# First modulation as rows in TensorE's column groups, later modulations held behind it, and an unused tile of 128 bytes

## The chip, the cores and the metric

The kernel runs on one core of a Trainium2 chip. The metric is the device time of one execution in microseconds (us), here as the median of three runs. Beside the runs, one execution was recorded by the hardware profiler; all durations below come from that record. Engines are called as in the profile: PE is TensorE, DVE is VectorE, ACT is ScalarE, POOL is GpSimd, SP is SyncE, whose queue issues the DMAs here.

## The reference

One layer of a decoder trunk, all in fp32, over 1024 positions of width 1024. A vector `c` gives six vectors that scale, shift and gate the two halves of the layer:

```python
cond = jax.nn.silu(c)
mod = cond @ ada_w[l] + ada_b[l]
sh1, sc1, g1, sh2, sc2, g2 = [m[:, None, :] for m in jnp.split(mod, 6, axis=-1)]
h = rmsnorm(x, ln1_g[l]) * (1 + sc1) + sh1
(a_val, a_gate, b_q, b_k, b_v, b_g, b_lr,
 c_q, c_k, c_v, d_u, d_v) = jnp.split(h @ w_in[l], splits, axis=-1)
...
mix = jnp.concatenate([o_a, o_b, o_c, o_d], axis=-1).astype(dt) @ w_out[l]
x = x + g1 * mix
h = rmsnorm(x, ln2_g[l]) * (1 + sc2) + sh2
x = x + g2 * conv_ffn(h, ffn_up[l], ffn_conv_w[l], ffn_conv_b[l], ffn_down[l])
return rmsnorm(x, lnf_g)
```

The four outputs `o_a` to `o_d` are a convolution of 31 taps, a gated linear attention, a dilated attention and a spatial gate; `conv_ffn` is an up-projection to 2 x 2816, a convolution of three taps, a gate and a down-projection. "The first modulation" below is the pair `sh1`, `sc1`; "the later ones" are the other four vectors.

## The kernel before

**Matrix products.** Each fp32 matrix is split into a high part, rounded to TensorE's fp32r format, and a low part, the rest (ACT makes the high part at L70, POOL or DVE the low one at L71). A product is then three fp32r matmuls: low x high, high x low, high x high (L92 to L94 in the first part of the kernel, L1221 to L1223 in `chain_mm` of the feed-forward part). `h_t` are tiles of 512 columns with activations or left operands, `wh_t` tiles with weights; in the feed-forward part `ht_t` are 24 further tiles of 512 columns that hold sums of blocks and the down-projection's operands. They are allocated in the pool `ph2`, and stand in a matmul either as the moving operand (`ht_t,wh_t` in a row's names) or as the weights of the array (`h_t,ht_t`).

**The start.** The eight row tiles of `x` are loaded in two halves (g = 0 and 1, four tiles each). `norm1` makes their squares' sums (ACT, two of the tiles on DVE), a reciprocal root by Newton steps on DVE (L77 to L82), and scales the rows (L249 on ACT, L251 on DVE). `norm1_T` transposes them on TensorE, a block of 128 columns at a time (L264), and ACT or DVE (L288) copies the transposed blocks to `xrT`. `modulate` then applies scale and shift: the high part `hH` straight on ACT (L318), the fp32 value in place (L322 on ACT for g = 0, L320 on DVE for g = 1), and the low part `hL` on POOL as their difference (L323). `first` multiplies `hH` and `hL` with the weights of the convolution and its gate (L331), 168 matmuls of 512 columns, accumulated over the eight blocks k as these come.

**The modulation.** Scale and shift of a block k are 128 elements each along the partitions. They are made in five pieces, `ADA_1` = (0), (1), (2, 3), (4, 5), (6, 7), so that the first blocks can start before the whole of `ada_w` is there. For a piece p, `ada_mac` multiplies blocks of `ada_w` by the elements of `cond` and adds them up on DVE (L222 for the first, L224 for the others), `ada_sum` sums the result over the partitions on TensorE with a column of ones as the moving operand (L304; for p = 0 the first four of the eight k go to TensorE directly, with a column of `cond`), and `ada_mod` adds the bias and one and multiplies by the norm's gain (L310 to L312). The order is written out by hand: `with after(...)` holds back what is queued inside it until a named instruction has been issued.

**The later modulations** are made by `ada_rest` with the same products on DVE (L826, L828), from 256-column blocks that share the buffers of tag `k2` with the accumulators of the first; a scheduler interleaves them with the projections. Two such accumulators are begun at 61.87 us, ahead of the convolution's taps on DVE (L464, L471).

## Time and profile before

| | us |
|---|---|
| median of three runs | 1170.57 |
| lowest and highest run | 1168.76, 1171.06 |
| the profiled execution | 1173.14 |
| its span | 1171.4 |
| TensorE busy | 1120.8 (96% of the span) |
| DVE busy | 810.9 (69%) |
| POOL busy | 707.6 (60%) |
| ACT busy | 561.8 (48%) |

The profiled execution took 1173.14 us, of which the span from the first to the last recorded instruction is 1171.4 us. Its mean granted clock of TensorE is 0.990 of full speed. TensorE is the busiest engine by far, and over the whole span the others have room; but these are means over parts with different limits, and in a short part at the start another engine can be the one that is full. In the rows below, the idle time in brackets is that of the engine just ahead of the row, and the arrow names what ended it.

### The profile page before, as it was taken

The numbers are of one execution on the slowest core, as the hardware profiler recorded it, in microseconds if no ns is written. First come the engines' busy times: TensorE is split into PE (matmuls) and PEld (weight loads), VectorE is DVE, ScalarE is ACT, GpSimd is POOL, SyncE is SP. The second block draws the span as 40 slices with busy tenths as digits, with TensorE's granted clock in tenths as the row PEclk, the third lists the DMA queues.
The fourth block names the chain that finished last, engine by engine and source line by source line (L and its number), as shares of the span: only waits on it lengthen the run. The fifth ranks groups of instructions, "written<-read, shape, count | busy, mean of one in ns | idle before, by whom it ended". The sixth has DMA issues, their size and how long they took to land.

```text
span 1171.4 us, 16065 instructions
## 1 busy us (share of the span) xinstructions
PE 1120.8 (96%) x5686; PEld 917.0 (78%) x5686; DVE 810.9 (69%) x1321; ACT 561.8 (48%) x909; POOL 707.6 (60%) x487
## 2 busy tenths in 40 slices
PE   4889999999999999999999999999999999999996
PEld 4668987866797878877887888888887778888885
DVE  6998979376678865555576676857686766654547
ACT  5552235373331523367666555555554646443432
POOL 2565574221232346648978777867787737895963
PEclk9999999989999999999999999999999999999998
DMA  9632232031331534482134546445644488574533
GB/s 354 253 100 71 75 112 86 19 108 58 123 109 64 188 99 180 153 293 76 46 135 135 189 180 242 172 168 183 242 181 178 144 308 329 194 239 142 198 109 144
DMA packets 70145, 186.86 MB, mean 160 GB/s; under 512 B 8097, under 2 KB 9265, under 8 KB 70065
## 3 DMA queue, kind: packets, MB, share of 16 engines
q1 hardware_dynamic: 70064, 185.84, 45.3%
q8 instruction: 45, 0.74, 0.2%
q14 instruction: 36, 0.29, 0.1%
HBM read 141.50 MB, written 42.21 MB: 157 GB/s over the span
## 4 chain that ended last, share of the span: by engine, by line
PE 71%; DVE 6%; POOL 2%; issue 2%; ACT 2%; DMA 2%; SPq 0%; ACTq 0%; DVEq 0%; POOLq 0%
PE a_ps L1221 8%; PE a_ps L1223 8%; PE a_ps L1222 8%; PE s_ps L92 4%; PE s_ps L93 4%; PE s_ps L94 3%; PE e_ps L1221 3%; PE e_ps L1222 3%; PE e_ps L1223 3%; PE y_ps L1223 3%; PE y_ps L1222 3%; PE y_ps L1221 3%; PE c_ps L1223 2%; PE c_ps L1221 2%; PE c_ps L1222 2%
## 5 line engine op out<-in xcount | busy, mean ns | idle before, releaser
L71 POOL TENSOR_TENSOR wh_t<-wf_t,wh_t 128x512 fp32r<-128x512 f32 (+2 forms) x131 | 216.4, 1659 | 178.6 <-ACT wh_t L70 169.3
L70 ACT CAST wh_t<-wf_t 128x512 fp32r<-128x512 f32 (+2 forms) x135 | 98.0, 739 | 139.7 <-PE s_ps L93 35.1
L1114 DVE SCALAR_TENSOR_TENSOR y_ps<-x_t,col,y_ps 128x1023 f32<-128x1023 f32 x88 | 112.6, 1283 | 38.9 <-ACT y_ps L1112 38.1
L71 POOL TENSOR_TENSOR h_t<-m_t,h_t 128x512 fp32r<-128x512 f32 x70 | 102.3, 1476 | 39.2 <-ACT h_t L70 37.3
L71 DVE TENSOR_TENSOR ht_t<-m_t,ht_t 128x512 fp32r<-128x512 f32 x65 | 80.1, 1245 | 65.3 <-ACT ht_t L70 63.5
L1387 ACT COPY x_t<-a_ps 128x512 f32<-128x512 f32 x81 | 47.4, 585 | 79.5 <-PE a_ps L1223 79.4
L471 DVE SCALAR_TENSOR_TENSOR s_ps<-m_t,col,s_ps 128x512 f32<-128x512 f32 (+19 forms) x116 | 80.3, 740 | 1.1
L70 ACT CAST ht_t<-m_t 128x512 fp32r<-128x512 f32 x65 | 40.3, 620 | 78.2 <-DMA m_t<-ps 20.7
L71 POOL TENSOR_TENSOR wh_t<-m_t,wh_t 128x512 fp32r<-128x512 f32 x52 | 67.2, 1305 | 16.5 <-ACT wh_t L70 16.1
L1221 PE MATMUL a_ps<-h_t,wh_t 128*128 128x512 f32 x188 | 73.7, 392 | 1.7 <-ACT x_t L1240 1.0
L828 DVE SCALAR_TENSOR_TENSOR acc<-ad,cond,acc 128x256 f32<-128x256 f32 x112 | 68.8, 622 | 8.8 <-DMA ad<-in_ada 7.3
L1223 PE MATMUL a_ps<-h_t,wh_t 128*128 128x512 f32 x188 | 73.3, 390 | 0.0
L1222 PE MATMUL a_ps<-h_t,wh_t 128*128 128x512 f32 x188 | 73.3, 390 | 0.0
L680 POOL TENSOR_TENSOR m_t<-m_t,mx 128x128 f32<-128x128 f32 (+7 forms) x16 | 19.3, 1206 | 85.2 <-DVE mx L678 82.9
L1221 PE MATMUL a_ps<-ht_t,wh_t 128*128 128x512 f32 x176 | 69.5, 395 | 0.0
L1223 PE MATMUL a_ps<-ht_t,wh_t 128*128 128x512 f32 x176 | 69.5, 395 | 0.0
L1222 PE MATMUL a_ps<-ht_t,wh_t 128*128 128x512 f32 x176 | 69.4, 394 | 0.0
L93 PE MATMUL s_ps<-wh_t,h_t 128*128 128x512 f32 (+1 forms) x192 | 69.2, 361 | 0.0
L94 PE MATMUL s_ps<-wh_t,h_t 128*128 128x512 f32 (+1 forms) x192 | 68.9, 359 | 0.0
L92 PE MATMUL s_ps<-wh_t,h_t 128*128 128x512 f32 (+1 forms) x192 | 65.6, 368 | 1.0 <-DVE g1b L837 1.0
L1221 PE MATMUL e_ps<-h_t,wh_t 128*128 128x512 f32 x148 | 57.9, 391 | 0.9 <-POOL wh_t L71 0.9
L1222 PE MATMUL e_ps<-h_t,wh_t 128*128 128x512 f32 x148 | 57.7, 390 | 0.0
(344 smaller groups left out, 3356.5 us busy)
## 6 DMA issues: line engine op xcount, KB each, us to landing
m_t<-in_ffn_up SPq DMA_DIRECT2D x46, 512.0 KB, 4.8
ad<-in_ada SPq DMA_DIRECT2D x64, 256.0 KB, 3.4
ps<-m_t SPq DMA_DIRECT2D x22, 512.0 KB, 7.3
x_t<-in_ffn_down SPq DMA_DIRECT2D x22, 512.0 KB, 6.8
m_t<-ps SPq DMA_DIRECT2D x33, 256.0 KB, 4.3
x_t<-in_x SPq DMA_DIRECT2D x16, 512.0 KB, 6.3
wf_t<-in_w_out SPq DMA_DIRECT2D x16, 512.0 KB, 3.6
m_t<-in_ffn_down SPq DMA_DIRECT2D x28, 256.0 KB, 5.4
```

Source lines behind the costliest of these rows:

```text
L70: ac.copy(dst_h, src)
L71: return eng.tensor_tensor(dst_l, src, dst_h.bitcast(F32), op=ALU.subtract)
L92: pe.matmul(ps, ll, rh, start=first, stop=False)
L93: pe.matmul(ps, lh, rl, start=False, stop=False)
L94: return pe.matmul(ps, lh, rh, start=False, stop=last)
L471: ve.scalar_tensor_tensor(yA[t][:, o + a:e] if last else y[:, a:], h[:, o + a - s:e - s], cc(O_CW + (CONV_K - 1 - s) * 2 + t), y[:, a:], o ...
L828: ve.scalar_tensor_tensor(acc, f[:, kk, :], cond[:, k:k + 1], acc, op0=ALU.mult, op1=ALU.add)
L1114: ve.scalar_tensor_tensor(y[:, n:], z[:, :S - n], cc(O_FW + 88 - 44 * n + f), y[:, n:], op0=ALU.mult, op1=ALU.add)
L1221: pe.matmul(ps, ll, rh, start=start, stop=False, skip_group_check=True)
L1222: pe.matmul(ps, lh, rl, start=False, stop=False, skip_group_check=True)
L1223: return pe.matmul(ps, lh, rh, start=False, stop=stop, skip_group_check=True)
L1387: ac.copy(dict(P1=lo(za[f]), P6=hi(za[f]), P7=hi(zb), P4=lo(zb))[p], ba)
```

## The change

Three things are changed, and one or two that go with them.

In the first, `ada_mac` and `ada_sum` are replaced by `ada_rows`. The vector `cond` is copied 64 times side by side (`condr`), and stands as the weights of the array: 64 columns for p = 0 and 1, 32 columns for p = 2 to 4. A block of `ada_w`, 128 columns, is the moving operand. The output of a product lies on 64 or 32 partitions, so two or four column groups of the array each take their own 128 columns of `ada_w` and write their own partitions of one PSUM tile; every row in a group is the same. DVE copies the 128 x 128 result (L226 of the changed kernel), TensorE transposes it (L227), and every 64th or 32nd column of the transposed tile is a vector of the modulation. All eight k are done so, for every p.

In the same part, the in-place operation of `modulate` for g = 0 goes from ACT to DVE, and every second copy of a transposed block goes to DVE in place of every fourth. In the second, the first product of a later modulation is held until the last instruction of the latest `ada_mod` has been issued. In the third, the pool `ph2` gets one tile of 128 bytes per partition that nothing uses, ahead of its other tiles; `ht_t` and the 1024-column tiles `m4_t` then begin at multiples of 256 bytes (before, 128 bytes past one). `h_t` and `wh_t` begin at multiples of 256 bytes in both kernels.

```diff
@@ -200,7 +200,6 @@
     xt = [t_x() for _ in range(NT)]
     ada_t = {}
     SQ = ((1, 2), (1, 3))
-    PM = (4, 0, 0, 0, 0)
 
     def ada_load(p):
         ada_t[p] = []
@@ -215,14 +214,19 @@
         return ada_t[p][k // nk][:, k % nk, :]
 
 
-    def ada_mac(p):
-        acc = accs[p] = sm1.tile([P, 512], F32, tag="k2", name="acc1", bufs=N_K2)[:, :256 * len(ADA_1[p])]
-        for k in range(PM[p], KT):
-            if k == PM[p]:
-                r = ve.tensor_scalar(acc, ada_block(p, k), cond[:, k:k + 1], None, op0=ALU.mult)
-            else:
-                r = ve.scalar_tensor_tensor(acc, ada_block(p, k), cond[:, k:k + 1], acc, op0=ALU.mult, op1=ALU.add)
-        mac_last[:] = [r.ins]
+    def ada_rows(p):
+        n = 2 * len(ADA_1[p])
+        m, o = P // n, p % 2 * P
+        row, rows_T = sum_ps[:, o:o + P], sum_ps[:, 256 + o:256 + o + P]
+        for k in range(KT):
+            for c in range(n):
+                pe.matmul(row[m * c:m * c + m, :], condr[:, k, :m], ada_block(p, k)[:, c * P:(c + 1) * P],
+                          start=k == 0, stop=k == KT - 1)
+        rs = sm1.tile([P, 256], F32, tag="k1", name="rows", bufs=4)[:, :P]
+        ve.tensor_copy(rs, row)
+        r = pe.transpose(rows_T, rs, ident)
+        mods[p] = rows_T[:, 0:P:m]
+        return r.ins
 
     W1 = Weights([(w_a[k], 1024) for k in range(4)] + [(w_feat[FEAT_COLS.index(C_AG + P)], 1024)]
                  + [(w_feat[1], 1024), (w_feat[2], 1024), (w_tok[2, 0], 1024), (w_tok[2, 1], 1024), (w_feat[3], 1024), (w_feat[4], 1024)]
@@ -238,6 +242,8 @@
         x_load(i)
     ada_load(2)
     ac.activation(cond, cc(O_C, 8), AF.Silu)
+    condr = sm1.tile([P, 512], F32, tag="k2", name="condr", bufs=N_K2).rearrange("p (k m) -> p k m", k=KT)
+    ve.tensor_copy(condr, cond.unsqueeze(2).broadcast_to([P, KT, 64]))
     ve.tensor_scalar(adab1[:, 0, :], cc(O_AB + 8, 8), 1.0, None, op0=ALU.add)
     ve.tensor_scalar(adab1[:, 1, :], cc(O_AB + 32, 8), 1.0, None, op0=ALU.add)
 
@@ -285,41 +291,26 @@
     def norm1_T(g, ks):
         for k in ks:
             tp = norm_T(xt[4 * g:4 * g + 4], k, p_s)
-            (ve.tensor_copy if k in (3, 7) else ac.copy)(xrT[k][:, half(g)], tp)
+            (ve.tensor_copy if k % 2 else ac.copy)(xrT[k][:, half(g)], tp)
 
 
     hH = [[None, None] for _ in range(KT)]
     hL = [[None, None] for _ in range(KT)]
-    accs = {}
-    mac_last = []
-
-    def ada_sum(p):
-        for n in range(2 * len(ADA_1[p])):
-            c = 2 * ADA_1[p][0] + n
-            cs = slice(n * P, (n + 1) * P)
-            ms_ = [(ada_block(p, k)[:, cs], cond[:, k:k + 1]) for k in range(PM[p])]
-            if p in accs:
-                ms_.append((accs[p][:, cs], ones[:, 0:1]))
-            for i, (w, v) in enumerate(ms_):
-                r = pe.matmul(sum_ps[:, c:c + 1], w, v, start=i == 0, stop=i == len(ms_) - 1)
-        return r.ins
+    mods, mod_last = {}, []
 
     def ada_mod(p):
         t0, n = ADA_1[p][0], len(ADA_1[p])
-        tp, ks = sum_ps[:, 2 * t0:2 * (t0 + n)], slice(t0, t0 + n)
+        tp, ks = mods[p], slice(t0, t0 + n)
         ve.tensor_tensor(mod[:, 1, ks], tp[:, 0:n], cc(O_AB + t0, n), op=ALU.add)
         ve.tensor_tensor(mod[:, 0, ks], tp[:, n:2 * n], adab1[:, 0, ks], op=ALU.add)
-        ve.tensor_tensor(mod[:, 0, ks], mod[:, 0, ks], cc(O_L1 + t0, n), op=ALU.mult)
+        mod_last[:] = [ve.tensor_tensor(mod[:, 0, ks], mod[:, 0, ks], cc(O_L1 + t0, n), op=ALU.mult).ins]
 
     def modulate(ks, g):
         for k in ks:
             hf = xrT[k][:, half(g)]
             hH[k][g], hL[k][g] = t_h(), t_h()
             r = ac.activation(hH[k][g], hf, AF.Identity, bias=mod[:, 1, k:k + 1], scale=mod[:, 0, k:k + 1])
-            if g:
-                ve.tensor_scalar(hf, hf, mod[:, 0, k:k + 1], mod[:, 1, k:k + 1], op0=ALU.mult, op1=ALU.add)
-            else:
-                r = ac.activation(hf, hf, AF.Identity, bias=mod[:, 1, k:k + 1], scale=mod[:, 0, k:k + 1])
+            ve.tensor_scalar(hf, hf, mod[:, 0, k:k + 1], mod[:, 1, k:k + 1], op0=ALU.mult, op1=ALU.add)
             gp.tensor_tensor(hL[k][g], hf, hH[k][g].bitcast(F32), op=ALU.subtract)
         return r
 
@@ -334,19 +325,15 @@
 
     sum_ps = p_s()
     ve.memset(sum_ps, 0.0)
-    scaled = norm1(0)
+    ada_rows(0)
+    norm1(0)
     norm1_T(0, range(2))
-    with after(scaled):
-        ada_mac(0)
-        W1.split()
-        with after(*mac_last):
-            ada_mac(1)
-    ada_sum(0)
+    W1.split()
     wk = W1.get()
     ada_mod(0)
     r0 = modulate(ADA_1[0], 0).ins
     a_ps = [[p_s(), None] for _ in range(4)]
-    with after(ada_sum(1)):
+    with after(ada_rows(1)):
         f0 = first(wk, ADA_1[0], 0)
     ada_mod(1)
     modulate(ADA_1[1], 0)
@@ -362,7 +349,7 @@
             first(wk, ks, 0)
         if p == 1:
             ks = (0, 1)
-            scaled = norm1(1, r0)
+            norm1(1, r0)
             norm1_T(1, range(KT))
             for ft in range(3):
                 a_ps[ft][1] = p_s()
@@ -372,9 +359,7 @@
         with tc.issue_after(rounded.ins):
             W1.split()
         if p + 1 < len(ADA_1):
-            with after(*mac_last) if p > 1 else after(scaled):
-                ada_mac(p + 1)
-            ada_sum(p + 1)
+            ada_rows(p + 1)
         first(wk, ks, 1)
     W1.split()
 
@@ -823,7 +808,8 @@
                 for kk in range(2):
                     k = q * 2 + kk
                     if k == 0:
-                        ve.tensor_scalar(acc, f[:, kk, :], cond[:, 0:1], None, op0=ALU.mult)
+                        with after(*mod_last):
+                            ve.tensor_scalar(acc, f[:, kk, :], cond[:, 0:1], None, op0=ALU.mult)
                     else:
                         ve.scalar_tensor_tensor(acc, f[:, kk, :], cond[:, k:k + 1], acc, op0=ALU.mult, op1=ALU.add)
             if bc is not None:
@@ -1246,6 +1232,7 @@
 
 
     raw, tok = {}, {}
+    ph2.tile([P, 32], F32, name="pad")
 
     def token_rows(n):
 
```

On TensorE, the start of the program before reads as follows (the first number of a shape is partitions, the second columns; x12 is the number of such in a row; an fp32 product by a column counts once here and is two instructions in the trace):

```order
L304 MATMUL s_ps<-cond,m_t 128x1 x4
L264 MATMUL s_ps<-ident,x_t 128x128 x8
L304 MATMUL s_ps<-ones,acc_169 128x1
L304 MATMUL s_ps<-cond,m_t 128x1 x4
L304 MATMUL s_ps<-ones,acc_169 128x1
L304 MATMUL s_ps<-ones,acc_180 128x1 x2
L331 MATMUL s_ps<-h_t,wh_t 128x512 x12
L264 MATMUL s_ps<-ident,x_t 128x128 x11
L331 MATMUL s_ps<-h_t,wh_t 128x512 x8
L264 MATMUL s_ps<-ident,x_t 128x128
L331 MATMUL s_ps<-h_t,wh_t 128x512 x4
L264 MATMUL s_ps<-ident,x_t 128x128 x44
```

In the changed kernel the same place reads:

```order
L223 MATMUL s_ps<-m_t,condr 64x128 x16
L270 MATMUL s_ps<-ident,x_t 128x128 x8
L227 MATMUL s_ps<-ident,rows 128x128
L223 MATMUL s_ps<-m_t,condr 64x128 x16
L227 MATMUL s_ps<-ident,rows 128x128
L322 MATMUL s_ps<-h_t,wh_t 128x512 x12
L270 MATMUL s_ps<-ident,x_t 128x128 x12
L322 MATMUL s_ps<-h_t,wh_t 128x512 x12
L223 MATMUL s_ps<-m_t,condr 32x128 x5
L270 MATMUL s_ps<-ident,x_t 128x128 x12
L223 MATMUL s_ps<-m_t,condr 32x128 x27
L270 MATMUL s_ps<-ident,x_t 128x128 x12
```

The eight transposes of the first two blocks stand between the two first modulations' pieces in both. The sums of `acc` are gone, and with them what TensorE waits for on DVE; in their place stand 16 products of `ada_w` and `condr` per piece, and the third piece's 32 are broken up by transposes. Further on, the pieces of the changed kernel lie between the first projections (L331 before, L322 now):

```order
L322 MATMUL s_ps<-h_t,wh_t 128x512 x22
L223 MATMUL s_ps<-m_t,condr 32x128 x8
L223 MATMUL s_ps<-x_t,condr 32x128 x4
L322 MATMUL s_ps<-h_t,wh_t 128x512 x4
L223 MATMUL s_ps<-x_t,condr 32x128 x4
L223 MATMUL s_ps<-m_t,condr 32x128
L322 MATMUL s_ps<-h_t,wh_t 128x512 x16
L223 MATMUL s_ps<-m_t,condr 32x128 x7
L223 MATMUL s_ps<-x_t,condr 32x128 x8
L322 MATMUL s_ps<-h_t,wh_t 128x512 x18
L227 MATMUL s_ps<-ident,rows 128x128
L223 MATMUL s_ps<-m_t,condr 32x128 x8
```

Counting from the start, products of `condr` stand in nine unbroken blocks.

On DVE, the later modulations' first products stood as follows before, among the modulations of the second half (L320) and the fifth `ada_mod` (L310 to L312):

```order
L224 SCALAR_TENSOR_TENSOR acc_561<-x_t,cond,acc_561 128x512 x2
L826 TENSOR_SCALAR acc_1352<-ad_1353,cond 128x256
L828 SCALAR_TENSOR_TENSOR acc_1352<-ad_1353,cond,acc_1352 128x256
L828 SCALAR_TENSOR_TENSOR acc_1352<-ad_1357,cond,acc_1352 128x256
L320 TENSOR_SCALAR m_t<-m_t,mod 128x512
L828 SCALAR_TENSOR_TENSOR acc_1352<-ad_1357,cond,acc_1352 128x256
L828 SCALAR_TENSOR_TENSOR acc_1352<-ad_1389,cond,acc_1352 128x256
L310 TENSOR_TENSOR mod<-s_ps,col 128x2
L320 TENSOR_SCALAR m_t<-m_t,mod 128x512
L311 TENSOR_TENSOR mod<-s_ps,adab_63 128x2
L828 SCALAR_TENSOR_TENSOR acc_1352<-ad_1389,cond,acc_1352 128x256
L312 TENSOR_TENSOR mod<-mod,col 128x2
```

Now they stand behind the fifth `ada_mod` (L304 to L306 of the changed kernel):

```order
L313 TENSOR_SCALAR m_t<-m_t,mod 128x512 x3
L226 COPY rows<-s_ps 128x128
L313 TENSOR_SCALAR m_t<-m_t,mod 128x512
L304 TENSOR_TENSOR mod<-s_ps,col 128x2
L305 TENSOR_TENSOR mod<-s_ps,adab_63 128x2
L306 TENSOR_TENSOR mod<-mod,col 128x2
L812 TENSOR_SCALAR acc_1432<-ad_1433,cond 128x256
L812 TENSOR_SCALAR acc_1567<-ad_1568,cond 128x256
L814 SCALAR_TENSOR_TENSOR acc_1432<-ad_1433,cond,acc_1432 128x256
L814 SCALAR_TENSOR_TENSOR acc_1567<-ad_1568,cond,acc_1567 128x256
L313 TENSOR_SCALAR m_t<-m_t,mod 128x512
L814 SCALAR_TENSOR_TENSOR acc_1432<-ad_1437,cond,acc_1432 128x256 x2
```

The two accumulators of the later modulations (`acc_1352` and `acc_1487` before, `acc_1432` and `acc_1567` now) begin behind the last `mod`, and are filled in turns; the taps of the convolution follow behind them in both.

## Rows read from the trace of the kernel before

**Rows 1.** By stretch: length, busy time of each engine, PEclk, DMA, GB/s.

```profile
25.40:46.40 21.00, 15.59 (x98) 12.63 (x97) 20.01 (x38) 12.61 (x21) 7.24 (x4) 0.99 0.67 251
46.40:84.20 37.80, 33.50 (x146) 26.81 (x146) 37.12 (x46) 19.59 (x25) 26.64 (x17) 0.96 0.41 142
84.20:1171.40 1087.20, 1061.30 (x5406) 868.55 (x5406) 739.09 (x1198) 516.03 (x845) 668.25 (x457) 0.99 0.44 153
sum 1171.40, PE 1120.79 PEld 917.02 DVE 810.95 ACT 561.82 POOL 707.60; mean PE 224.16 PEld 183.40 DVE 162.19 ACT 112.36 POOL 141.52
```

**Rows 2.** Timeline of TensorE, 0 to 45 us: start, length, instruction, count, idle before.

```profile
21.59 1.01 PE L304 MATMUL s_ps<-ones,acc 128*128 128x1 f32 x4 [3.15 <-DVE acc L224]
22.47 4.36 PE L331 MATMUL s_ps<-h_t,wh_t 128*128 128x512 f32 x12
...
32.28 2.00 PE L264 MATMUL s_ps<-ident,x_t 128*128 128x128 f32 x16 [0.92 <-DVE m_t L288]
35.11 3.14 PE L264 MATMUL s_ps<-ident,x_t 128*128 128x128 f32 x24 [0.84 <-DVE m_t L288]
```

**Rows 3.** Timeline of TensorE, 45 to 92 us.

```profile
46.40 6.87 PE L331 MATMUL s_ps<-h_t,wh_t 128*128 128x512 f32 x23 [3.53 <-ACT h_t L318]
...
60.56 2.79 PE L331 MATMUL s_ps<-h_t,wh_t 128*128 128x512 f32 x11 [2.04 <-ACT h_t L318]
...
80.15 3.02 PE L331 MATMUL s_ps<-h_t,wh_t 128*128 128x512 f32 x12 [1.28 <-POOL h_t L323]
84.14 0.50 PE L92 MATMUL s_ps<-h_t,wh_t 128*128 128x512 f32 x1 [0.98 <-POOL wh_t L71]
```

**Rows 4.** Timeline of ACT, 26 to 50 us.

```profile
45.53 0.81 ACT L318 ACTIVATE h_t<-m_t,mod 128x512 fp32r<-128x512 f32 x1 [5.45 <-DVE mod L312]
```

**Rows 5.** Busy time of line 224 on DVE, 0 to 85 us.

```profile
0.00:85.00 85.00, 29.76 (x31) 0.98 0.63 237
```

**Rows 6.** Timeline of TensorE, two products of twelve matmuls, first and last of each.

```profile
604.38 0.39 PE L1221 MATMUL a_ps<-h_t,wh_t 128*128 128x512 f32 x1
...
606.87 0.39 PE L1223 MATMUL a_ps<-h_t,wh_t 128*128 128x512 f32 x1
...
701.57 0.40 PE L1221 MATMUL a_ps<-ht_t,wh_t 128*128 128x512 f32 x1
...
704.13 0.39 PE L1223 MATMUL a_ps<-ht_t,wh_t 128*128 128x512 f32 x1
```

**Rows 7.** Busy time of line 304 on PE and PEld, 0 to 85 us.

```profile
0.00:85.00 85.00, 8.41 (x48) 8.43 (x48) 0.98 0.63 237
```

**Rows 8.** Timeline of TensorE, 185 to 208 us, line 715.

```profile
185.17 0.44 PE L715 MATMUL s_ps<-pt,m_t 128*64 128x128 f32 x4
...
198.03 0.88 PE L715 MATMUL s_ps<-pt,m_t 128*64 128x128 f32 x12
```

**Rows 9.** Timeline of TensorE, 312.8 to 314.5 us.

```profile
312.89 0.28 PE L410 MATMUL s_ps<-wh_t,h_t 128*128 128x256 f32 x1
313.10 1.09 PE L715 MATMUL s_ps<-pt,m_t 128*64 128x128 f32 x14
314.12 0.39 PE L411 MATMUL s_ps<-wh_t,h_t 128*128 128x256 f32 x1
```

**Rows 10.** Groups by line, 0 to 110 us: count, busy us, mean ns.

```profile
L828 DVE SCALAR_TENSOR_TENSOR acc<-ad,cond,acc 128x256 f32<-128x256 f32 x14 | 11.7, 836 | 0.4
...
L320 DVE TENSOR_SCALAR m_t<-m_t,mod 128x512 f32<-128x512 f32 x8 | 5.6, 694 | 0.0
```

**Rows 11.** Groups by line of TensorE, 500 to 1171.4 us.

```profile
L1223 PE MATMUL a_ps<-h_t,wh_t 128*128 128x512 f32 x188 | 73.3, 390 | 0.0
...
L1223 PE MATMUL a_ps<-ht_t,wh_t 128*128 128x512 f32 x176 | 69.5, 395 | 0.0
...
L1223 PE MATMUL y_ps<-h_t,ht_t 128*128 128x512 f32 x132 | 52.1, 395 | 0.0
```

**Rows 12.** Busy time of PE, PEld, DVE, ACT, POOL with tile ht_t.

```profile
500.00:1171.40 671.40, 419.35 (x1764) 331.23 (x1764) 112.45 (x97) 58.56 (x97) 2.59 (x2) 1.00 0.52 184
```

## The prediction

> **What bounds the kernel now.** I read the stretches of the trace first. In the column of TensorE (PE) the reader is to see that it leaves 50.6 us of the 1171.4 us idle, that after 84.20 us it is busy for 1061.30 of 1087.20 us, and that half of the idle time lies ahead of that point [rows 1]. From 84.20 us on (the first projection behind the modulated norm) the kernel is bound by TensorE's own instructions; a change can pay there by fewer or shorter matmuls, and ahead of 84.20 us by letting TensorE get through the norm, the modulations and the first projections sooner. A gain ahead of 84.20 us is carried nearly whole to the end, since the 25.9 us of idle behind it are all that could swallow a part.
>
> Next comes TensorE's timeline up to 84 us, where the reader is to see the brackets with the idle time: 3.15 us behind the modulation products of DVE (L224), 0.92 and 0.84 us behind DVE's copies of transposed blocks (L288) [rows 2], then 3.53 and 2.04 us behind the modulated tiles of ACT (L318), 1.28 us behind POOL's low parts (L323), and 0.98 us behind the weight split [rows 3]. Together these are 12.7 us. What stands behind the 3.53 us is in ACT's timeline: its first modulated tile of that stretch had waited 5.45 us for DVE's `mod` (L312) [rows 4]. So the scale and shift of a norm come too late because DVE makes them: it is busy for 20.01 of 21.00 us from 25.40, and for 37.12 of 37.80 us from 46.40 [rows 1]; 29.8 us of its time up to 85 us are the 31 multiply-adds of `ada_mac` [rows 5].
>
> **The clock.** The granted clock from 46.40 to 84.20 us is 0.96 [rows 1]; TensorE's levels are full (2.4 GHz) and half (1.2 GHz), so some 3 us of that stretch ran at half, right behind the 3.53 us of idle, and cost 1.5 us. In the first stretch the first twelve L331 took 4.36 us [rows 2], where twelve at the full clock take 12 x 0.226 = 2.7 us (the step of a 512-column matmul, from the 12 in a row with `h_t` in [rows 6]); some 1.4 us of that is the clock again, since TensorE had stood 3.15 us ahead of them. With the idle time gone I take both back: 12.7 + 2.9 = **15.6 us** that the first part can win.
>
> **The change, part by part.** *Rows for columns.* Removed from TensorE: 48 short instructions (L304), 8.4 us [rows 7]. Added: 128 fp32 products, and an fp32 product is two instructions here (before, 24 of them were the 48 of [rows 7]), so 256 instructions with 128 columns moving: 32 and 32 in two column groups, 192 in four. No such row with four groups exists. The nearest is the product of attention's weights with the values (L715), in two groups of 64: from 4 to 12 of them the time grows by 0.44 us, 0.055 us each [rows 8]; a full-width 128-column one (the transposes of L264) took 2.00 us for 16 [rows 2], 0.125 at most, 0.11 without the run-out of the last. So two groups halve it. Four should at best halve it again, 0.027, and at worst give no more than two, 0.055; I take 0.041, between. Modulation 0 is made when TensorE has just begun, where the slow level is likely: 32 x 0.109 = 3.5 us (1.8 at full). Modulation 1: 32 x 0.055 = 1.8. The others: 192 x 0.041 = 7.9 (5.2 to 10.6). Entering and leaving the groups costs something too: between the L410 at 312.89 and the L411 at 314.12 lie 1.23 us, of which 14 x 0.055 + 0.12 (a normal step of that line) explain 0.89 [rows 9]; 0.34 us are left for one block. The order of the changed kernel has nine such blocks in this part: 3.1 us. The five transposes with their way in and out I put at 0.2 us each, 1.0. Added: 3.5 + 1.8 + 7.9 + 3.1 + 1.0 = **17.3 us**.
>
> The Trainium skill, "TensorEngine Tiling (Array Packing)", section Key Properties, says that a change of tiling mode drains TensorE, which speaks against rows that the scheduler breaks into nine blocks. The 0.34 us of [rows 9] agree with it. The skill's "TensorE: Matmul & The Clock Gate", Part 3, gives 2.38 times for three column tiles at once; by that rate four groups would take about 0.035 to 0.046 us each (an estimate), 6.7 to 8.8 us for the 192. Without it the bounds above stand.
>
> *DVE.* It loses the 31 multiply-adds and five first multiplies of `ada_mac`, 29.8 us for the former [rows 5]. It gains one copy of `cond`, five short copies of rows, four block copies more and eight modulations of g = 0 that ACT had (0.694 each, 5.6 us) [rows 10]. So DVE gives back some 20 us in the stretch where it was full. The 16 products for the later modulations (14 at 0.836 us, 11.7 us [rows 10], and two first ones) move behind the fifth `mod`, where they stand ahead of the convolution's taps; since 20 us have gone from ahead of them, I have them done no later than before, at no cost. If that cover is gone, the waits that grow are those of the later modulations' sums and of the convolution.
>
> *What is late next.* With `mod` ready earlier, the second half of the norm is late: its four rows wait for the squares on ACT and the root on DVE, which the change does not shorten. The waits behind L288 of [rows 2] lie there, and I let 1.5 us of the 15.6 remain. First part: 15.6 + 8.4 - 17.3 - 1.5 = **5.2 us** gained.
>
> *The tile of 128 bytes.* It is never used; it moves the tiles that are allocated behind it in this pool, and brings `ht_t` from 128 past a multiple of 256 bytes to such a multiple. `h_t` and `wh_t` are at multiples in both kernels. The reader is to compare products of one shape: twelve matmuls with `h_t` and `wh_t` have their starts 2.49 us from first to last; twelve with `ht_t` moving 2.56 [rows 6], which is 6.4 ns more for each of the 11 steps. The mean duration is 390 ns with `h_t` and `wh_t`, 395 with `ht_t` moving, and 395 with `ht_t` as weights [rows 11]: 5 ns, in both roles. The trace has 1764 matmuls with `ht_t` [rows 12]. By the starts they give up to 11.3 us, by the durations 8.8. I take 5.2 ns, close to the durations, since those are means over hundreds: **9.2 us**. No row shows that the address is the reason. The tiles differ in their place too, and the copies to `ht_t` on other engines are not slower than those to others; so the lower bound is nothing.
>
> **Sum.** The profiled execution took 1173.14 us, 1.7 more than its span and 2.6 more than the median of the runs, 1170.57. 1173.14 - 5.2 - 9.2 = 1158.7; less 2.6, **1156** us as a median.
>
> **The rivals.**
> - *The address is not the cause.* For it: the last paragraph's objection. Against: both roles show the same excess [rows 11]. Then only the first part pays: 1170.6 - 5.2 = **1165**.
> - *DVE is late behind the held products.* DVE was full up to 84 us [rows 1]; the 16 products now stand in one block ahead of the convolution, and loads that need their buffers wait with them. If 4 to 5 us of this reach TensorE, only the tile pays: **1161**. Against: the 20 us taken from DVE.
> - *Neither pays*: **1170**, no change to be measured.
> - *Four groups do not work side by side.* Then each of the 192 costs 0.109: 20.9 us in place of 7.9, and the first part loses 7.8: **1178** if the tile does nothing, 1169 if it pays. It decides from 0.068 us for one of the 192 (13.0 us for all); the rows at two groups say 0.055, so four must be worse than two.
>
> **How the numbers follow.** Both parts pay 0.50 (1156, own range 1150 to 1161); only the first 0.25; the tile alone, or with a part of the first, 0.10; neither 0.07; four groups in series 0.08, of which 0.02 with a tile that pays. A measurement of this kernel tells about 0.2%, 2.3 us, from no change. Faster: 0.50 + 0.25 + 0.10 = 0.85; same: 0.07 + 0.02 = 0.09; slower 0.06. The range goes from the upper bound of the tile with four groups at 0.027 (1171 - 8 - 11, rounded) to the first part alone with 3 us lost of it: **1150 to 1168**; outside lie neither, the series and the tails, some 0.2.
>
> **What would show it.** The first projection (L92) starts at about 79 us in place of 84.14, and the idle time behind L318 and DVE's products is gone; the rows with 32 columns out lie 0.027 to 0.055 us apart (0.109 would be the last rival); DVE is less than nine tenths busy from 25 to 75 us, and the convolution starts no later than before. Twelve matmuls with `ht_t` span 2.49 us as those with `h_t`, and their mean duration falls by some 5 ns; if it stays, the address was not the cause. The prediction is wrong if TensorE waits for the held products' sums between 84 and 200 us, or if the clock stays at half through the rows and the first projections.

## The result, and the profile after

The changed kernel takes 1158.95 us in the median of eight runs (1156.24 to 1164.65); the kernel before, on the same chip, 1170.52 us (1167.86 to 1174.15, eight runs). The ratio is 0.9896 with a 95% interval of 0.9875 to 0.9917: 11.6 us faster, inside the range of the prediction (1150 to 1168) and 3 us above its point. The profiled execution took 1163.19 us, so its profile is one of the slower ones of this kernel, 4.2 us above the median.

First TensorE's timeline at the start, answering to [rows 2, 3]; the columns are those of there.

```profile
10.31 3.68 PE L223 MATMUL s_ps<-m_t,condr 128*64 128x128 f32 x32 [10.31 <-DMA m_t<-in_ada]
...
16.55 1.97 PE L223 MATMUL s_ps<-m_t,condr 128*64 128x128 f32 x32 [0.81 <-DVE mod L305]
19.75 0.33 PE L227 MATMUL s_ps<-ident,rows 128*128 128x128 f32 x1 [1.23 <-DVE rows L226]
19.83 3.02 PE L322 MATMUL s_ps<-h_t,wh_t 128*128 128x512 f32 x12
...
28.88 1.73 PE L223 MATMUL s_ps<-m_t,condr 128*32 128x128 f32 x54
...
52.35 0.65 PE L223 MATMUL s_ps<-m_t,condr 128*32 128x128 f32 x16 [0.32 <-DVE mod L305]
...
73.23 0.41 PE L92 MATMUL s_ps<-h_t,wh_t 128*128 128x512 f32 x1
```

Here the reader is to see three things. The first projection (L92) starts at 73.23 us in place of 84.14: 10.9 us sooner, where the prediction had 5.2. The waits behind DVE's products, ACT's tiles and POOL's low parts are gone; what is left between 10.31 and 73.23 us are waits of 0.81, 1.23 and 0.32 us. And the first twelve of the projection's matmuls take 3.02 us, not 4.36.

The stretches, answering to [rows 1] (the same columns):

```profile
25.40:46.40 21.00, 20.91 (x192) 16.03 (x190) 15.39 (x33) 11.13 (x15) 12.13 (x8) 1.00 0.94 356
46.40:73.20 26.80, 26.48 (x196) 21.05 (x196) 15.36 (x27) 10.12 (x13) 16.24 (x11) 1.00 0.35 118
73.20:1161.50 1088.30, 1056.13 (x5410) 870.91 (x5409) 753.26 (x1209) 515.81 (x847) 674.35 (x458) 0.99 0.45 153
```

TensorE now has no gap worth naming from 25.4 to 73.2 us, at the full clock (1.00), and DVE, which was full there, is busy for 15.39 of 21.00 and 15.36 of 26.80 us. But the third row holds 32.2 us of idle TensorE, where [rows 1] had 25.9 in a part that is the same work. Some of the gain was given back there.

The feed-forward products by line, answering to [rows 11]:

```profile
L1209 PE MATMUL a_ps<-h_t,wh_t 128*128 128x512 f32 x187 | 72.8, 389 | 0.0
...
L1209 PE MATMUL y_ps<-h_t,ht_t 128*128 128x512 f32 x132 | 51.3, 389 | 0.0
...
L1209 PE MATMUL c_ps<-ht_t,wh_t 128*128 128x512 f32 x88 | 34.2, 389 | 0.0
...
L1209 PE MATMUL a_ps<-ht_t,wh_t 128*128 128x512 f32 x176 | 69.2, 393 | 0.0
```

Products with `ht_t`, moving or as weights, now last as long as the others, 389 ns in place of 395, wherever TensorE ran at the full clock. The last row, the largest of them, reads 393 because some of its matmuls stood in a stretch at half the clock (0.50 granted from 926.6 to 933.4 us), where each took 0.63 us. A second profile of the same kernel, without that stretch (the run `changed_again` below), has 389 for it:

```profile
L1209 PE MATMUL a_ps<-ht_t,wh_t 128*128 128x512 f32 x176 | 68.5, 389 | 0.0
```

Where did it go? TensorE's waits over the whole span (columns: who waits for whom, us in total, times, the longest):

```profile
PE e_ps L1207 <- POOL wh_t L71: 5.0, 3, 1.7
```

The kernel before had 0.9 us of this kind, once. The first feed-forward product starts at 498.70 us, 8.2 us sooner than the 506.86 of before, and the span ends at 1161.5 us, 9.9 sooner than 1171.4: of the 9 to 10 us that `ht_t` saves in this part, 1.7 show in this execution. Part of the rest is the clock: from 900 to 950 us the granted clock is 0.93, where the kernel before has 1.00 from 500 to 1165 us. The second profile (1159.78 us, near the median) has 1.00 there and 4.9 us of the same three waits; from its first feed-forward product (497.56 us) to its end (1158.1) it takes 4.0 us less than the kernel before.

### The profile page after: what moved, and what is told of

It reads as the page before. It is cut to its first block, busy times and chain, and to the rows that moved or that the text cites. A ratio compares the mean times of both kernels' runs of the same rounds, so it can differ in the third digit from the quotient of the medians.

```text
span 1161.5 us, 16450 instructions
## 1 busy us (share of the span) xinstructions
PE 1116.6 (96%) x5899; PEld 919.4 (79%) x5899; DVE 796.6 (69%) x1303; ACT 551.7 (48%) x897; POOL 709.3 (61%) x487
## 4 chain that ended last, share of the span: by engine, by line
PE 57%; DVE 13%; DMA 7%; issue 3%; ACT 2%; POOL 2%; SPq 1%; ACTq 0%; DVEq 0%; POOLq 0%
DMA x_t<-in_ffn_down 6%; PE a_ps L1207 6%; PE a_ps L1209 5%; PE a_ps L1208 5%; PE s_ps L92 4%; PE s_ps L93 3%; PE s_ps L94 3%; PE y_ps L1209 3%; PE y_ps L1208 3%; PE y_ps L1207 3%; DVE y_ps L1100 2%; PE e_ps L1207 2%; PE e_ps L1209 2%; PE e_ps L1208 2%; PE c_ps L1209 2%
## 5 line engine op out<-in xcount | busy, mean ns | idle before, releaser
L1100 DVE SCALAR_TENSOR_TENSOR y_ps<-x_t,col,y_ps 128x1023 f32<-128x1023 f32 x88 | 112.7, 1284 | 39.1 <-ACT y_ps L1098 38.2
L456 DVE SCALAR_TENSOR_TENSOR s_ps<-m_t,col,s_ps 128x512 f32<-128x512 f32 (+26 forms) x116 | 80.6, 744 | 1.2
L814 DVE SCALAR_TENSOR_TENSOR acc<-ad,cond,acc 128x256 f32<-128x256 f32 x112 | 72.1, 656 | 7.5 <-DMA ad<-in_ada 6.3
L1207 PE MATMUL a_ps<-h_t,wh_t 128*128 128x512 f32 x188 | 73.9, 393 | 2.3 <-ACT x_t L1226 1.0
L1209 PE MATMUL a_ps<-h_t,wh_t 128*128 128x512 f32 x188 | 73.2, 390 | 0.0
L1208 PE MATMUL a_ps<-h_t,wh_t 128*128 128x512 f32 x188 | 73.2, 389 | 0.0
L1207 PE MATMUL a_ps<-ht_t,wh_t 128*128 128x512 f32 x176 | 69.6, 395 | 0.0
L92 PE MATMUL s_ps<-wh_t,h_t 128*128 128x512 f32 (+1 forms) x192 | 66.2, 373 | 0.8 <-DVE g1b L823 0.8
L1207 PE MATMUL e_ps<-h_t,wh_t 128*128 128x512 f32 x148 | 58.3, 394 | 5.5 <-POOL wh_t L71 5.0
```

What stands on the lines that cost most here:

```text
L92: pe.matmul(ps, ll, rh, start=first, stop=False)
L456: ve.scalar_tensor_tensor(yA[t][:, o + a:e] if last else y[:, a:], h[:, o + a - s:e - s], cc(O_CW + (CONV_K - 1 - s) * 2 + t), y[:, a:], o ...
L814: ve.scalar_tensor_tensor(acc, f[:, kk, :], cond[:, k:k + 1], acc, op0=ALU.mult, op1=ALU.add)
L1100: ve.scalar_tensor_tensor(y[:, n:], z[:, :S - n], cc(O_FW + 88 - 44 * n + f), y[:, n:], op0=ALU.mult, op1=ALU.add)
L1207: pe.matmul(ps, ll, rh, start=start, stop=False, skip_group_check=True)
L1208: pe.matmul(ps, lh, rl, start=False, stop=False, skip_group_check=True)
```

## The experiments

The change has two parts that can be taken apart, the start and the tile. The first four kernels ask what each is worth, whether the hold is needed, and whether an order of POOL's is behind the 5.0 us.

**The tile alone** (on the kernel before):

```diff
     raw, tok = {}, {}
+    ph2.tile([P, 32], F32, name="pad")
```

> The kernel before with the unused tile alone; nothing of the start changed. If the address is the cause (ht_t off a multiple of 256 bytes), the mean duration of the 1764 matmuls with ht_t falls from 395 to 389 or 390 ns and their step from 233 to 227, which takes 9 us off TensorE; POOL's splits in the feed-forward part may give back up to 5 us, so 1161 to 1166 us, a ratio of 0.992 to 0.996. Rival (the place in memory or the operand, not the address modulo 256): steps stay at 233 ns, ratio 0.999 to 1.001.

Measured: 1167.48 us, ratio 0.9970 (0.9958 to 0.9983). TensorE's groups in this kernel:

```profile
L1223 PE MATMUL y_ps<-h_t,ht_t 128*128 128x512 f32 x132 | 51.3, 389 | 0.0
...
L1223 PE MATMUL c_ps<-ht_t,wh_t 128*128 128x512 f32 x88 | 34.2, 389 | 0.0
```

The durations fall as expected, 128 bytes do it, and the rival as I had put it (steps stay) is out. (The groups of `a_ps` with `ht_t` read 391 to 396, with some of their matmuls at half the clock.) But only 3.5 us reach the end, between the two ranges: 4.3 us of waits of `e_ps` behind POOL's splits, and stretches at half the clock (0.98 granted from 850 to 900 us, 0.92 from 900 to 950), are new here.

**The start alone** (the changed kernel without the tile):

```diff
     raw, tok = {}, {}
-    ph2.tile([P, 32], F32, name="pad")
```

> The changed kernel without the unused tile, so the start alone. If the two parts are independent: the first projection starts near 73 us as in the changed kernel, the steps with ht_t are back at 233 ns, and the gain that is left at the end of the attention part (8.4 us in the changed kernel's profile) reaches the end: 1161 to 1163 us, ratio 0.992 to 0.994. Rival (a gain in the start is swallowed by later waits, and the tile made all of the result): ratio 0.998 or more.

Measured: 1167.66 us, ratio 0.9964 (0.9944 to 0.9983). Its first projection starts at 73.42 us and its first feed-forward product 11.9 us sooner than before, yet 3 to 4 us of this reach the median, again between the two ranges. In its feed-forward part, which runs the same instructions in the same order as before, TensorE waits for 4.4 us behind POOL's splits. By the medians the two parts alone give 3.4 and 3.3 us; together 11.6.

**The hold** (the changed kernel without it):

```diff
-                        with after(*mod_last):
-                            ve.tensor_scalar(acc, f[:, kk, :], cond[:, 0:1], None, op0=ALU.mult)
+                        ve.tensor_scalar(acc, f[:, kk, :], cond[:, 0:1], None, op0=ALU.mult)
```

> The changed kernel without the hold on the later modulations' first products. If the hold is needed to keep DVE free for the modulations, the products go back among them, the modulated tiles come later, and the first projection starts 1 to 4 us later than at 73.2: ratio 0.991 to 0.994. Rival (DVE has room once its sums are gone, the hold is worth nothing): the first projection within 0.5 us of 73.2, ratio 0.989 to 0.991.

Measured: 1165.17 us, ratio 0.9945 (0.9929 to 0.9961); the first projection starts at 82.14 us. TensorE's and DVE's timelines of this kernel:

```profile
69.58 12.72 PE L322 MATMUL s_ps<-h_t,wh_t 128*128 128x512 f32 x42 [4.54 <-ACT h_t L312]
```

```profile
61.31 4.98 DVE L813 SCALAR_TENSOR_TENSOR acc<-ad,cond,acc 128x256 f32<-128x256 f32 x7
67.19 0.48 DVE L813 SCALAR_TENSOR_TENSOR acc<-ad,cond,acc 128x256 f32<-128x256 f32 x1 [0.90 <-DMA ad<-in_ada]
67.59 0.15 DVE L304 TENSOR_TENSOR mod<-s_ps,col 128x2 f32<-128x2 f32 x1
```

Without the hold the later modulations' products stand ahead of the fifth `ada_mod` on DVE, one even waits for a load there, and TensorE waits 4.54 us for the tile that needs it; half the clock follows (68.9 to 75.8 us). The hold is worth 9 us at the first projection and some 6 at the end. I had 1 to 4.

**POOL's sums later** (the changed kernel with the sums for the next weights behind a split):

```diff
-            gp.tensor_tensor(s1, lo(b), hi(b), op=ALU.add)
-            gp.tensor_tensor(s2, s1, lo(a), op=ALU.subtract)
+            with after(*p3_last):
+                gp.tensor_tensor(s1, lo(b), hi(b), op=ALU.add)
+                gp.tensor_tensor(s2, s1, lo(a), op=ALU.subtract)
...
-        split(*ops[f, p], src, gp)
+        q = split(*ops[f, p], src, gp)
+        if p == "P3":
+            p3_last[:] = [q.ins]
+
+    p3_last = []
```

> The changed kernel with one order more: in the feed-forward part POOL's sums of the next weights (L1189, L1190), which wait for a load, are put behind the split for the product P3 of the present ones. If these sums in front of the split make TensorE wait (e_ps behind POOL's wh_t, 5.0 us in the changed kernel's profile against 0.9 before), the wait is gone and the time falls by 3 to 6 us: ratio 0.984 to 0.987. Rival (the split is late because of ACT's cast or of the buffers, or the half clock is by itself): ratio 0.989 to 0.991, and TensorE waits elsewhere for as long.

Measured: 1157.97 us, ratio 0.9885 (0.9867 to 0.9903). The waits of `e_ps` are gone from its profile, but the median is only 1 us below that of the changed kernel, inside both intervals, and some of the waiting has moved: TensorE waits 1.5 us behind a split for `a_ps` (0.6 before the move), and 3.4 us behind DVE's `ht_t` (2.4). Whether the two orders differ was put to the other three kernels, with the changed one again beside them, on another chip:

> The kernel before with the sums (L1203, L1204) behind the split for P3, nothing else. If that order only costs once TensorE runs ahead (0.9 us of such waits in the profile of before), it gives 0 to 2 us here: ratio 0.998 to 1.000. Rival (the order costs the kernel before as much as the others): 4 to 5 us, 0.996.

> The start alone (no unused tile) with the sums behind the split. If the start's gain is lost by the splits that come behind the sums (waits of 4.4 us there in its profile), it comes back: the 10 to 11 us that the first projection is earlier reach the end less 1 to 3 us, ratio 0.991 to 0.993 (without the moved sums 0.9964). Rival (the gain is lost elsewhere, in the attention part or by the clock): 0.995 to 0.997.

> The tile alone with the sums behind the split. If the 9 us that the faster ht_t matmuls take off are lost behind the sums (waits of 4.3 us and the half clock behind them), they come back: ratio 0.992 to 0.994 (without the moved sums 0.997). Rival (faster matmuls just wait more elsewhere): 0.996 to 0.998.

> The changed kernel itself, unaltered, beside the three others on one chip: ratio 0.988 to 0.992 again, first projection near 73 us. By the waits of its first profile (5.0 us behind POOL's splits) it should lie 1 to 4 us above the same kernel with the sums moved.

| kernel | as it is | with the sums later |
|---|---|---|
| before | 1 | 1.0037 (1.0023 to 1.0052) |
| tile alone | 0.9970 (0.9958 to 0.9983) | 0.9973 (0.9960 to 0.9986) |
| start alone | 0.9964 (0.9944 to 0.9983) | 0.9945 (0.9927 to 0.9962) |
| both | 0.9896 (0.9875 to 0.9918), again | 0.9885 (0.9867 to 0.9903) |

Each ratio is against the kernel before on the same chip; the left column's second and third rows and the right column's last come from one chip, the other four from another.

My theory of POOL's order falls. With the other order the kernel before gets 4 us slower (its profiled execution took 1171.69 us, 3.6 below its median, and does not show why), the tile alone the same, and the start alone perhaps 2 us faster. What the right column does show is that there the parts add up: the tile gives 0.0064 (7.5 us) without the start and 0.0060 (7.0) with it, the start 0.0092 (10.8) without the tile and 0.0088 (10.3) with it. Those are close to the 9 and the 10.9 us that the profiles show at the source. In the left column the first of the two gives 3.5 us (the tile) or 4.2 (the start) and the second 8 or 8.7: the kernel before is some 4 us better off than the parts would have it, and either edit loses that. Each ratio has an interval of some 2 us to either side, and the 4 us come of three of them, so they are likely rather than certain; the profiles of the left column point the same way, with 0.9 us of waits behind POOL's splits in the kernel before and 4.3, 4.4 and 5.0 in the others.

**Where the feed-forward part loses.** The three waits of 5.0 us in the changed kernel's profile are of one pattern. Here is the one at 853 us, on DVE, ACT, POOL and PE, each in a fence of its timeline:

```profile
839.81 0.89 DVE L1143 TENSOR_TENSOR x_t<-x_t 128x512 f32<-128x512 f32 x1 [4.98 <-DMA x_t<-in_ffn_down]
840.62 0.68 DVE L1385 TENSOR_TENSOR x_t<-e_ps,x_t 128x512 f32<-128x512 f32 x1
841.22 1.18 DVE L1145 TENSOR_TENSOR x_t<-x_t 128x512 f32<-128x512 f32 x1
842.44 1.67 DVE L1147 TENSOR_TENSOR x_t<-x_t 128x512 f32<-128x512 f32 x1
844.14 1.67 DVE L1149 TENSOR_TENSOR x_t<-x_t 128x512 f32<-128x512 f32 x1
845.72 2.60 DVE L1100 SCALAR_TENSOR_TENSOR y_ps<-x_t,col,y_ps 128x1023 f32<-128x1023 f32 x2
848.23 0.69 DVE L1380 TENSOR_TENSOR x_t<-c_ps,x_t 128x512 f32<-128x512 f32 x1
848.83 1.22 DVE L1111 TENSOR_TENSOR y_ps<-x_t,y_ps 128x1024 f32<-128x1024 f32 x1
```

```profile
850.09 1.01 ACT L1113 COPY x_t<-y_ps 128x1024 f32<-128x1024 f32 x1 [6.43 <-DVE y_ps L1111]
850.99 0.62 ACT L70 CAST wh_t<-m_t 128x512 fp32r<-128x512 f32 x1
```

```profile
851.69 1.26 POOL L71 TENSOR_TENSOR wh_t<-m_t,wh_t 128x512 fp32r<-128x512 f32 x1 [3.49 <-ACT wh_t L70]
```

```profile
853.01 0.50 PE L1207 MATMUL e_ps<-h_t,wh_t 128*128 128x512 f32 x1 [1.74 <-POOL wh_t L71]
```

Read backwards: TensorE waits for POOL's low part of a weight; POOL for ACT's high part; ACT's cast stands behind its copy of the gated product (L1113), which waits 6.43 us for DVE; and DVE has the four sums of the down-projection's weights (`weight_sums`, L1143 to L1149) ahead of the convolution (L1100) and gate (L1111). The sums are slow where POOL is busy beside them: an addition of the same size with an operand in PSUM takes 0.68 us (L1385), these up to 1.67. The Trainium skill's page "SBUF — State Buffer", section "SBUF: two separate sides", has it that of a VectorE operation with two inputs in SBUF and a GpSimd operation that reads SBUF, the one that starts first holds the other up for its whole length. The rows agree, with 1.67 us for a sum beside a split and 0.68 or 0.69 for one alone.

The first row of DVE's fence belongs to this too: DVE had waited 4.98 us for the load of the weights that it sums (`in_ffn_down`). That load is issued behind the stores of the products gated one round before, so gate, load, sums and gate form a loop. The chain of work that ended last shows it (start, length, what; columns of that view):

```profile
832.06 8.56 DMA x_t<-in_ffn_down
841.22 1.19 DVE x_t L1145
842.44 1.68 DVE x_t L1147
844.14 1.67 DVE x_t L1149
...
848.92 1.15 DVE y_ps L1111
850.09 1.02 ACT x_t L1113
...
852.96 7.75 DMA x_t<-in_ffn_down
```

From 666 to 869 us these loads are 34.1% of that chain in the changed kernel (26.1% in its second profile). In the kernel before the same stretch of the chain is TensorE's matmuls, although DVE waits as long for its load there (4.88 us at 847.14 us). So the loop was a little shorter than TensorE's work before, and the TensorE that comes sooner and runs faster meets it.

How a round of the loop gets longer can be read from the start alone, whose rows up to there are those of the kernel before, 11.8 us earlier. First a round of the kernel before, then the same of the start alone:

```profile
693.50 0.69 DVE L1398 TENSOR_TENSOR x_t<-e_ps,x_t 128x512 f32<-128x512 f32 x1 [0.18 <-DMA x_t<-in_ffn_down]
694.11 0.68 DVE L1159 TENSOR_TENSOR x_t<-x_t 128x512 f32<-128x512 f32 x1
...
701.22 1.22 DVE L1125 TENSOR_TENSOR y_ps<-x_t,y_ps 128x1024 f32<-128x1024 f32 x1
```

```profile
681.65 0.69 DVE L1384 TENSOR_TENSOR x_t<-e_ps,x_t 128x512 f32<-128x512 f32 x1 [0.18 <-PE e_ps L1209]
682.98 1.42 DVE L1145 TENSOR_TENSOR x_t<-x_t 128x512 f32<-128x512 f32 x1 [0.63 <-DMA x_t<-in_ffn_down]
...
690.83 1.22 DVE L1111 TENSOR_TENSOR y_ps<-x_t,y_ps 128x1024 f32<-128x1024 f32 x1
```

The second sum waits 0.63 us for its load, starts behind POOL's split (682.56 us) in place of ahead of it (694.40 before, the sum at 694.11), and takes 1.42 us in place of 0.68; the lead falls from 11.85 us to 10.39 at the gate. In the changed kernel the gate (L1111) is 10.2 us ahead of that before (L1125) at 669 us and 6.5 at 750, where four rounds with sums lie between, and again 9.7 at 785 and 4.5 at 868. By line, the third sum took this long on average in the kernel before and in the changed one (at 853 us itself it is as long in both, 1.68 and 1.67):

```profile
L1161 DVE TENSOR_TENSOR x_t<-x_t 128x512 f32<-128x512 f32 x11 | 14.4, 1314 | 0.4
```

```profile
L1147 DVE TENSOR_TENSOR x_t<-x_t 128x512 f32<-128x512 f32 x11 | 18.3, 1666 | 0.4
```

**Without the sums of weights** (a kernel for the question alone):

```diff
         yield 1
-        ve.tensor_tensor(lo(we), hi(we), lo(we), op=ALU.subtract)
         yield 1
-        ve.tensor_tensor(hi(we), hi(wo_), hi(we), op=ALU.subtract)
         yield 1
-        ve.tensor_tensor(hi(wo_), hi(wo_), lo(we), op=ALU.subtract)
         yield 1
-        ve.tensor_tensor(lo(wo_), lo(wo_), hi(wo_), op=ALU.subtract)
         yield 1
```

> The changed kernel with the four DVE sums of weight_sums (L1143 to L1149, 44 instructions, 54 us of DVE in its profile) left out, so that the down-projection's sums of weights are not made and the output is another. If these sums, stretched where POOL works at the same time (0.68 us alone, up to 1.67), hold up the gate, its store, and so the load that POOL waits for, then POOL's wait for the load (14.5 us) falls under 4 us, TensorE's wait behind POOL's split (5.0 us) is gone, and the ratio falls to 0.984 to 0.987. Rival (POOL is late by itself): the waits stay, 0.988 to 0.991.

Measured: 1153.03 us, ratio 0.9845 (0.9831 to 0.9860): 6 us below the changed kernel. ACT's copy in its timeline:

```profile
841.02 1.02 ACT L1113 COPY x_t<-y_ps 128x1024 f32<-128x1024 f32 x1 [1.26 <-DVE y_ps L1111]
```

It waits 1.26 us in place of 6.43, there is no wait of `e_ps` behind POOL in its list of waits, and the products with `ht_t` are at 389 or 390 ns (but for 394 of the first line of `a_ps<-h_t,ht_t`, which waits for its operand). POOL still waits 6.2 us for its load (I had under 4), which therefore costs nothing. So the loop through DVE's sums is what holds TensorE up in the changed kernel's feed-forward part; the load that I had suspected first, POOL's, does not. This kernel leaves out DVE's wait for the weights together with the sums, so it gives the worth of the loop and not of either piece. The kernel before was not run without its sums: that it loses less to the loop is read from its waits (0.9 us) and its chain alone.

**Two moves of the start undone** (modulation of g = 0 back on ACT, every fourth copy on DVE):

```diff
-            (ve.tensor_copy if k % 2 else ac.copy)(xrT[k][:, half(g)], tp)
+            (ve.tensor_copy if k in (3, 7) else ac.copy)(xrT[k][:, half(g)], tp)
...
-            ve.tensor_scalar(hf, hf, mod[:, 0, k:k + 1], mod[:, 1, k:k + 1], op0=ALU.mult, op1=ALU.add)
+            if g:
+                ve.tensor_scalar(hf, hf, mod[:, 0, k:k + 1], mod[:, 1, k:k + 1], op0=ALU.mult, op1=ALU.add)
+            else:
+                r = ac.activation(hf, hf, AF.Identity, bias=mod[:, 1, k:k + 1], scale=mod[:, 0, k:k + 1])
```

> The changed kernel with two of its moves undone: the in-place modulation of g = 0 is back on ACT, and only every fourth copy of a transposed block is on DVE. If these moves carry part of the gain (ACT was on the path: its modulated tiles are what TensorE waited for), the first projection is 1 to 4 us later than 73.2 us and the ratio 0.991 to 0.994. Rival (the gain is all from the rows and from DVE's 31 products that are gone): within 0.5 us, 0.989 to 0.991.

Measured: 1160.01 us, ratio 0.9905 (0.9891 to 0.9919), not told from the changed kernel. The first projection starts at 76.14 us, 2.9 later than 73.23, behind POOL's weight split:

```profile
76.14 0.50 PE L92 MATMUL s_ps<-h_t,wh_t 128*128 128x512 f32 x1 [1.54 <-POOL wh_t L71]
```

The changed kernel waits for the split behind that one (at 81.00 us, 1.43 us long), and this kernel does not: its matmul with the same number, the 25th of these products, starts at 81.71 us, 0.7 later and not 2.9. So these moves bring the projection forward by 3 us, and the next split takes most of it back: they carry nothing to the end that this measurement tells.

**Which address.** Two kernels ask what it is about 256 bytes: a tile of 64 bytes in the changed kernel (`ht_t` 192 past a multiple), and the kernel before with 128 bytes in the first pool (`h_t`, `wh_t` 128 past a multiple, `ht_t` at one).

```diff
-    ph2.tile([P, 32], F32, name="pad")
+    ph2.tile([P, 16], F32, name="pad")
```

> The changed kernel with a tile of 64 bytes in place of 128, so that ht_t begins 192 bytes past a multiple of 256. If only multiples of 256 are fast, the steps with ht_t are at 232 or 233 ns as before and the ratio is near that without a tile, 0.994 to 0.998. If multiples of 64 do, they are at 227 and the ratio 0.988 to 0.992.

```diff
     ms = cst.tile([P, NT], F32, name="ms")
+    cst.tile([P, 32], F32, name="pad")
```

> The kernel before with the 128 bytes in the first pool, ahead of everything: h_t, wh_t and the others that were at multiples of 256 bytes are now 128 past one, and ht_t comes to a multiple. If the address modulo 256 is the cause, the matmuls with h_t and wh_t (some 2200 of 512 columns without ht_t) go from 227 to 232 or 233 ns, 11 to 13 us slower, and those with ht_t, whose partner is now off, stay at 232 or 233 or more: ratio 1.008 to 1.013. Rival (something else in the place of ht_t): ht_t faster or all as before, 0.99 to 1.001.

Measured: 1164.72 us, ratio 0.9948 (0.9933 to 0.9964), and 1172.79 us, ratio 1.0024 (1.0006 to 1.0042). First groups with 64 bytes, then the timeline of TensorE with 128 in the first pool:

```profile
L1209 PE MATMUL c_ps<-ht_t,wh_t 128*128 128x512 f32 x88 | 34.7, 394 | 0.0
...
L1207 PE MATMUL y_ps<-h_t,ht_t 128*128 128x512 f32 x132 | 51.2, 388 | 0.0
L1208 PE MATMUL y_ps<-h_t,ht_t 128*128 128x512 f32 x132 | 51.7, 392 | 0.0
L1209 PE MATMUL y_ps<-h_t,ht_t 128*128 128x512 f32 x132 | 52.0, 394 | 0.0
```

```profile
659.84 0.39 PE L1222 MATMUL e_ps<-h_t,wh_t 128*128 128x512 f32 x1
...
660.97 0.39 PE L1224 MATMUL e_ps<-h_t,wh_t 128*128 128x512 f32 x1
661.20 0.40 PE L1222 MATMUL a_ps<-ht_t,wh_t 128*128 128x512 f32 x1
...
663.76 0.39 PE L1224 MATMUL a_ps<-ht_t,wh_t 128*128 128x512 f32 x1
```

64 bytes help little: the products with `ht_t` moving stay at 394 ns, and those with `ht_t` as weights are slow in part, 388, 392 and 394 ns by line. The time of the second kernel lies between the two ranges, and it refutes my rule as I had put it: products of `h_t` and `wh_t`, both 128 bytes past a multiple of 256, step by 226 ns (1.13 us for five), no slower than at multiples, while those of `ht_t`, now at a multiple, with `wh_t`, now off, step by 233 (2.56 us for eleven). So in the layouts 128 bytes apart a product is slow where its moving operand and its weights begin at different places modulo 256 (0 and 128, 128 and 0), and fast where they begin at the same one (0 and 0, 128 and 128): it is the two operands against each other, not either by itself. With 64 bytes this does not cover all: with `ht_t` moving (192 against 0) all three lines are slow, with `ht_t` as weights (0 against 192) L1207 is as fast as any. What tells L1207 from the other two lines there was not tried.

## Why the prediction came out as it did

**The bound of the start: right.** The idle time that it listed went as it said, 12.7 us, and two waits that it had not listed went too, 1.12 us ahead of the first transposes (13.32 us) and 0.36 behind `acc` (15.72 us). The 1.5 us left for new waits stand against 0.81 + 1.23 + 0.32. The clock gave back 2.6 of the 2.9 us: the projection's 168 matmuls (L331, now L322) had 43.7 us in their group and have 41.1. The half clock at the first twelve did not come of the 3.15 us of waiting, as the prediction had it: in the kernel before the eight transposes at 13.32 us take 2.03 us and the eleven at 26.66 us 1.36, so by its steps TensorE was at the half level ahead of that wait already (PEclk, which reads 1.00 there, does not show it).

**The cost of the rows: too high; this is the largest part of what made 10.9 out of 5.2.** The 256 instructions in their nine blocks took 12.73 us, ways in and out included:

```profile
0.00:85.00 85.00, 12.73 (x256) 10.23 (x256) 1.00 0.66 251
```

I had 16.3 (3.5 + 1.8 + 7.9 + 3.1), and 17.3 with the transposes; that is 3.6 of the 5.7 us missing. Four groups are the lower bound of my range, not its middle: 54 of them in 1.73 us, the last one's own 0.28 taken off, is 0.027 us each. The first block (32 in 3.68 us, twice the step of the second) and the second (32 in 1.97) were right. Rivals with groups in series are out. By the rate of the Trainium skill's "TensorE: Matmul & The Clock Gate", Part 3 (2.38 times for three column tiles), four would have been some 0.035 to 0.046 us, an estimate; the measurement decides, four groups give four times. Of the other 2.1 us, 1.5 are the two waits not listed, some 0.8 three matmuls of the projection that now stand behind the first L92 (77.59 us), and 0.5 the transposes of L264 (now L270); the new waits take 0.9 off. These are sums of groups that overlap a little.

**DVE: right, with the hold.** It had room from 25 us on; without the hold it would not have had it where it counts, which I had not worked out. The held products cost nothing: both accumulators begin at 62.18 us (61.87 and 73.61 before), the first tap of the convolution starts at 77.69 us (81.50 before), and TensorE's wait for the later modulations' sums is 1.6 us as before.

**The tile: right in its size, wrong in its rule.** 9.2 us by 5.2 ns was the forecast; 395 to 389 ns on 1764 matmuls is some 10 us at the source. The address was the cause, but as a difference between operands, and the 64 bytes show that the difference alone is not the whole of it.

**"A gain ahead of 84.20 us is carried nearly whole to the end": this step failed.** I took the idle time that stood behind that point as all that could swallow a part. Waits that were not there came up: 1.43 us at the weight split at 81 us, and in the feed-forward part three (5.0 us) behind the loop of load, DVE's sums, gate, ACT's copy and POOL's split, which hardly showed as idle time of TensorE before (0.9 us) because it was just short enough. 10.9 and some 9 to 10 us at the source made 11.6. That the point fitted is luck: the first term was half its size and the carriage was taken as whole, and the two errors nearly cancel. The rival that a DVE late behind the held products takes a part did not come true: it was other work of DVE, 760 us later.

**Left open.** Why the kernel before is some 4 us better off than the other three of the left column is shown for one round of one of them (the start alone, at 682.98 us) and otherwise argued: its sums of weights fell better against POOL's work (1314 ns against 1666). Why the load of that sum lands 0.6 us later there, and why the sums' other order costs the kernel before 4 us, isn't settled. And what in the hardware makes two operands' offsets matter was not tried.

## What to carry to other kernels

Idle time that stands in a profile does not bound what a gain can lose: before forecasting that TensorE's time is carried through a later loop, follow that loop's chain of producers backwards (here POOL, ACT, DVE, and a load that waits for the round before) and see how much lead it has. A vector by a matrix, wanted along the partitions, is cheaper as rows in column groups than as multiply-adds on a full DVE, and what could slide into the freed place has to be held back. Where products of the same shape take different times, compare the addresses of their operands with each other, and lay them out alike.

## What the hardware showed that I had not expected

A 512-column matmul stepped by 226 or 227 ns where both operands began at the same place modulo 256 bytes, and by 232 or 233 on average where they were 128 bytes apart, whichever operand was off. With 64 bytes between them it was slow with `ht_t` moving (394 ns) and slow in two of three lines with `ht_t` as weights (388, 392, 394). Four column groups of 32 took a quarter of a full-width matmul's time each (0.027 us against about 0.11). What is left of the 12.73 us, over the nine blocks, is an estimated 0.26 us for the way in and out of one: (12.73 - 32 x 0.107 - 32 x 0.055 - 192 x 0.027) / 9, with 0.107 from the first block, (3.68 - 0.35) / 31. I had estimated 0.34.
